# The last chunk of both output projections as a plain product by token blocks, in a diffusion block kernel

## The chip, the core and the metric

One core of a Trainium2 chip runs the whole program. The metric is the device time in microseconds of one execution; lower is better. TensorE (PE) multiplies, VectorE (DVE) and ScalarE (ACT) work on elements and on the accumulators in PSUM, GpSimd (POOL) works on elements in SBUF, and SyncE (SP) issues all transfers.

## What is computed

A block with 1024 latent tokens and 256 context tokens of width 1024, weights shared, modulation per token kind:

```
x = x + 0.5 * gate1 * swiglu(modulate(rmsnorm(x)), ff1_in, ff1_out)     # latent and context
mixer: one input projection, gated linear attention and gated MLP, one output projection
x = x + gate * mixer(modulate(rmsnorm(x)))                              # context only feeds states
x = x + 0.5 * gate2 * swiglu(modulate(rmsnorm(x)), ff2_in, ff2_out)     # latent only
out = rmsnorm(x) * final_g

def swiglu(y, w_in, w_out):
    gate, up = split(y @ w_in)
    return (silu(gate) * up) @ w_out                                    # 1024 -> 2 x 2816 -> 1024
```

## The kernel before

All values lie with features on the 128 partitions and tokens along the free axis: x[dt][tb] is feature tile dt (of 8) and token block tb (blocks 0 and 1 of 512 latent tokens, block 2 of 256 context tokens). Each operand of a product is split into a high and a low part in fp32r (an ACT copy and a subtraction, `split`, `hl`, `unit`), and each product is three matmuls: high by high, high by low, low by high.

Both products of an FFN are done by Winograd's variant of Strassen's scheme in 2 x 2 blocks: seven products instead of eight (`winograd`, products numbered 1, 2, 5, 7, 6, 3, 4). The rows of the left side are two halves of the weight (in the output projection feature tiles m and m + 4), the columns of the right side are token blocks 0 and 1, and the inner index is cut in two. `unit` (line 372) loads two weight tiles and makes the seven left operands with additions and subtractions on DVE (hidden part) or POOL (output projection). `combos` (L408 to L421) makes the combined right operands with four subtractions; `hl` (L429, L430) splits each.

`ffn` runs 22 hidden jobs first. `Hidden.end` finishes a pair of hidden tiles, and each pair's seven right operands are stored to DRAM (`hd`, L581). The output projection then reads them back (`hc`, L702) in CHUNKS of 1, 2, 2, 2, 2 and 2 pairs; each chunk has four jobs, one for each m. `Out.p1`, `p2`, `mid` and `end` add the products into sums in SBUF: `acc` for each feature tile and token block (L512), `us[m]` for the product that three of the four sums share. Up to the chunk before the last, product 6 goes to `us`, which `end` adds to the three sums there; in the last chunk it is added to each of the three directly. In the last chunk `finish` (L625) multiplies a sum by the gate and adds x, which it loads, and `tail` (`squares`, L461 and L463) squares the result on ACT and adds the square on DVE. So x of any token block is complete only when the last job has ended. In the first FFN the context's 256 tokens are a plain product in each job (`ctx`, L524 to L526), for two of the four jobs of the last chunk after all else.

After the first FFN `run` sums the squares over partitions for both blocks at once (`rstd_cols`: matmuls with ones, L265; a reciprocal square root in twelve small DVE steps, L279 and L247 to L255), spreads the result over the partitions (`spread`, L288) and norms block 0, block 1 and the context (`norm`: L327 on DVE, L329 and L331 on ACT, L334 on DVE or L332 on POOL). The mixer's products (L356 to L359) read the results. After the second FFN the same sums lead to sixteen outputs (L1399 and L1400 on ACT and POOL, or L1402 on DVE), which go to the result by L1404.

The order of instructions on each engine is worked out when the program is built: a planner takes instructions by priority (mostly the order of the code, `high_priority` earlier) as its own model of durations says that they are ready. At run time each engine works its list in order, and each waits for its operands. Buffers come from small pools: 32 of 1024 columns (`d`), 8 (`m`), 6 (`w`), 7 of 512 columns (`h`), and eight PSUM banks (`pg` 3, `po` 3, `pn` 2).

## Time and profile before

| what | value |
|---|---|
| time, median of 3 runs | 2215.16 us (2211.38 to 2219.64) |
| profiled execution, its own time | 2211.94 us |
| its span, first to last instruction | 2210.2 us |
| mean granted clock of PE | 0.951 of full speed |
| PE, DVE, ACT, POOL busy | 94%, 71%, 37%, 19% of the span |

The span is what the trace shows; 1.7 us of the execution's time lie around it. Times in the trace are counted from the start of the span. The first FFN's output projection ends at some 921 us, the mixer begins there, the second FFN's hidden part ends at some 1957 and its projection at 2180.

### The profile page before, as it was taken

How to read it: one execution, taken by the hardware profiler on the slowest of the kernel's cores; microseconds unless marked ns; L12 is line 12 of the kernel's file. 1: busy time of each engine (PE TensorE's matmuls, PEld its weight loads, DVE VectorE, ACT ScalarE, POOL GpSimd, SP SyncE). 2: the span in 40 equal slices, each digit the busy share in tenths (PEclk: the TensorE clock that was granted, in tenths of full speed). 3: DMA queues.
4: the chain of work that ended last, by engine and by line, in shares of the span. 5: the costliest groups of instructions: out<-in, count | busy, mean ns of one | idle time of the engine just before them, and what ended most of it. 6: DMA issues, size and time to landing. Idle time of an engine off the chain costs nothing.

```text
span 2210.2 us, 27546 instructions
## 1 busy us (share of the span) xinstructions
PE 2074.9 (94%) x10308; PEld 1722.6 (78%) x10308; DVE 1560.1 (71%) x2575; ACT 828.6 (37%) x1311; POOL 420.8 (19%) x245
## 2 busy tenths in 40 slices
PE   6799999999999999698999999996999999989995
PEld 2688888888878888577898787775788888867874
DVE  3976566666565689879877267779777776855587
ACT  3633333334351111275444234326344343441222
POOL 0000000000046565232111100110000000065772
PEclk9799999999999999899999986898999999999997
DMA  7033333233469776401111133541334343468851
GB/s 279 34 115 137 121 119 115 115 136 151 153 249 369 272 293 234 156 11 67 39 58 53 68 128 120 181 156 63 144 136 179 123 181 133 179 259 342 304 196 76
DMA packets 115878, 345.05 MB, mean 156 GB/s; under 512 B 12961, under 2 KB 15777, under 8 KB 115745
## 3 DMA queue, kind: packets, MB, share of 16 engines
q1 hardware_dynamic: 115744, 343.30, 42.2%
q8 instruction: 81, 1.33, 0.2%
q14 instruction: 53, 0.43, 0.1%
HBM read 237.87 MB, written 105.38 MB: 155 GB/s over the span
## 4 chain that ended last, share of the span: by engine, by line
PE 72%; DVE 15%; DMA 5%; POOL 3%; issue 3%; ACT 2%; SPq 0%; POOLq 0%; DVEq 0%; ACTq 0%
PE c L479 14%; PE a L479 13%; PE f L479 13%; PE b L479 7%; DVE acc L741 3%; PE sc L1056 2%; PE gc L526 2%; PE gc L525 2%; PE gc L524 2%; DVE acc L512 2%; DMA ar<-in_wb 1%; PE row L205 1%; PE st L265 1%; PE ogu L358 1%; PE ogu L356 1%
## 5 line engine op out<-in xcount | busy, mean ns | idle before, releaser
L384 POOL TENSOR_TENSOR gl<-raw,gh 128x1024 fp32r<-128x1024 f32 x22 | 54.1, 2461 | 1143.9 <-ACT gh L389 1129.6
L389 ACT ACTIVATE gh<-raw 128x1024 fp32r<-128x1024 f32 x66 | 70.0, 1060 | 198.6 <-PE c L479 83.7
L168 DVE SCALAR_TENSOR_TENSOR junk<-ar,cr 128x512 bf16<-128x512 f32 x160 | 111.9, 700 | 35.4 <-DMA ar<-in_wb 26.3
L393 ACT ACTIVATE sh<-s 128x1024 fp32r<-128x1024 f32 x66 | 69.7, 1057 | 170.8 <-PE a L479 93.2
L429 ACT ACTIVATE hl<-g 128x512 fp32r<-128x512 f32 x110 | 67.5, 626 | 158.8 <-DVE g L512 152.2
L479 PE MATMUL f<-hl,uh 128*128 128x512 f32 x528 | 126.8, 389 | 0.0
L479 PE MATMUL c<-hl,sh 128*128 128x512 f32 x352 | 110.9, 392 | 11.4 <-ACT hl L429 9.2
L479 PE MATMUL a<-hl,gh 128*128 128x512 f32 x352 | 113.6, 400 | 8.1 <-ACT hl L429 5.6
L479 PEld LDWEIGHTS f<-hl,uh 128*128 128x128 f32 x528 | 99.1, 188 | 20.6
L479 PE MATMUL b<-hl,gh 128*128 128x512 f32 x352 | 111.5, 393 | 1.0 <-ACT hl L429 1.0
L479 PE MATMUL f<-hl,th 128*128 128x512 f32 x352 | 110.1, 390 | 1.3 <-ACT hl L429 1.3
L479 PE MATMUL a<-hl,sh 128*128 128x512 f32 x352 | 110.2, 393 | 1.0 <-ACT g L552 1.0
L479 PE MATMUL c<-hl,th 128*128 128x512 f32 x352 | 109.0, 391 | 0.1
L741 DVE SCALAR_TENSOR_TENSOR acc<-z,par,acc 128x945 f32<-128x945 f32 (+2 forms) x64 | 95.5, 1511 | 12.0 <-ACT acc L763 10.9
L512 DVE TENSOR_TENSOR u<-c,u 128x512 f32<-128x512 f32 x44 | 30.3, 689 | 98.4 <-ACT u L562 98.4
L430 DVE TENSOR_TENSOR hl<-g,hl 128x512 fp32r<-128x512 f32 x110 | 76.9, 715 | 32.3 <-ACT hl L429 32.2
L142 POOL TENSOR_TENSOR wl<-raw,wh 128x1024 fp32r<-128x1024 f32 x20 | 52.3, 2614 | 222.5 <-ACT wh L141 213.7
L479 PEld LDWEIGHTS c<-hl,sh 128*128 128x128 f32 x352 | 66.2, 189 | 26.7 <-ACT hl L429 9.8
L384 DVE TENSOR_TENSOR sl<-s,sh 128x1024 fp32r<-128x1024 f32 x44 | 53.9, 1224 | 45.7 <-PE gc L525 21.9
L479 PEld LDWEIGHTS a<-hl,gh 128*128 128x128 f32 x352 | 66.6, 193 | 22.1 <-ACT hl L429 6.1
L512 DVE TENSOR_TENSOR acc<-f,acc 128x512 f32<-128x512 f32 x88 | 60.3, 688 | 28.3 <-PE f L479 23.0
L479 PEld LDWEIGHTS b<-hl,gh 128*128 128x128 f32 x352 | 67.0, 190 | 15.7 <-ACT hl L429 1.8
(330 smaller groups left out, 6211.6 us busy)
## 6 DMA issues: line engine op xcount, KB each, us to landing
hd<-hl SPq DMA_DIRECT2D x154, 512.0 KB, 3.7
hc<-hd SPq DMA_DIRECT2D x154, 512.0 KB, 7.7
ar<-in_wb SPq DMA_DIRECT2D x112, 256.0 KB, 3.1
raw<-in_ff1i SPq DMA_DIRECT2D x44, 512.0 KB, 3.8
raw<-in_ff2i SPq DMA_DIRECT2D x44, 512.0 KB, 4.7
raw<-in_ff1o SPq DMA_DIRECT2D x22, 512.0 KB, 6.2
raw<-in_ff2o SPq DMA_DIRECT2D x22, 512.0 KB, 5.4
raw<-in_wa SPq DMA_DIRECT2D x16, 512.0 KB, 10.0
```

The lines of the kernel that those rows point to most:

```text
L142: eng.tensor_tensor(out=lo[:, :n], in0=src[:, :n], in1=hi[:, :n].bitcast(F32), op=ALU.subtract)
L168: i = nc.vector.scalar_tensor_tensor(out=self.junk, in0=w, scalar=1.0, in1=cbc[j], op0=ALU.mult, op1=ALU.mult, accum_out=acc[:, h, dt, j:j ...
L384: sub = lambda o, x, y: eng.tensor_tensor(out=o, in0=x, in1=y, op=ALU.subtract)
L389: nc.scalar.activation(gh, g, AF.Copy)
L393: nc.scalar.activation(sh, s, AF.Copy)
L429: nc.scalar.activation(t[:, :512], src, AF.Copy)
L430: nc.vector.tensor_tensor(out=t[:, 512:], in0=src, in1=t[:, :512].bitcast(F32), op=ALU.subtract)
L479: mm = lambda x, y, start, stop: nc.tensor.matmul(ps, x, y, start=start, stop=stop, skip_group_check=more)
L512: tt = lambda eng, o, x, y, op: eng.tensor_tensor(out=o, in0=x, in1=y, op=op)
L524: nc.tensor.matmul(ps, hi[:, c], mh, start=i == 0, stop=False)
L525: nc.tensor.matmul(ps, hi[:, c], ml, start=False, stop=False)
L741: self.nc.vector.scalar_tensor_tensor(out=o, in0=zv[:, r0 + dr:r1 + dr, c0 + dc:c1 + dc], scalar=self.par[:, tap:tap + 1], in1=o, op0=ALU. ...
```

## The change

Three things are changed in both FFNs. The last chunk (hidden pairs 9 and 10) leaves the Winograd scheme: `last` multiplies it plainly, all eight feature tiles for token block 0, then all eight for block 1, then, in the first FFN, the context. Its weights are only split into high and low parts (`halves`), its right operands are the four blocks themselves, so that pairs 9 and 10 store four operands instead of seven and make no combinations. The sums of the other chunks are multiplied by the gate and added to x before the last chunk or in its first half (`finish` and `fold_u` for block 0 in the chunk before the last, for block 1 among block 0's tiles), and each tile of the last chunk is multiplied by the gate and added to x from PSUM (`more`). After each token block its own norm follows (`done`): in the first FFN the mixer's norm of that block, in the second the final norm and the outputs. x is loaded and its copy stored by pairs of feature tiles for each block. The sums' tiles hold two feature tiles of one block instead of one feature tile of both.

```diff
+    def halves(self, src, eng, new):
+
+        nc = self.nc
+        r = {}
+        for x, (i, j) in zip(src, ((1, 2), (0, 4))):
+            x = self.load(x)
+            hi, lo = new("vh", F32R), new("vl", F32R)
+            with self.tc.high_priority():
+                nc.scalar.activation(hi, x, AF.Copy)
+                eng.tensor_tensor(out=lo, in0=x, in1=hi.bitcast(F32), op=ALU.subtract)
+            r[i], r[j] = (hi[:, :512], lo[:, :512]), (hi[:, 512:], lo[:, 512:])
...
+        def tail(dt, tb):
+            sq = self.sv("sq") if tb in accs else self.tile(self.sb, 512, "ar", "acc")
+            nc.scalar.activation(sq, self.x[dt][tb], AF.Square)
+            if tb in accs:
+                nc.vector.tensor_tensor(out=accs[tb], in0=accs[tb], in1=sq, op=ALU.add)
+            else:
+                accs[tb] = sq
...
+        pairs0 = NF // 2 - CHUNKS[-1]
...
+                    if pair >= pairs0:
+                        out(5, b12)
+                        out(7, b22)
+                        return
                     layer.combos(b11, b12, b21, b22, out)
...
             def p2(s, b):
-                i = add(s.acc(s.m, 0), b, False)
+                i = add(xsum(s.m, 0), b, False)
                 if after_out:
                     after_out(s.j, i)
-                if s.last:
-                    s.finish(s.m, 0)
+                if s.fold:
+                    finish(s.m, 0)
                 if yc:
-                    if s.put_off:
-                        later.append(s.ctx)
-                    else:
-                        s.ctx()
+                    s.ctx()
 
             def mid(s, a, c, f):
                 m = s.m
                 if s.one:
                     us[m] = layer.h("u")
-                if s.last:
-                    for dt, tb in ((m + 4, 1), (m, 1), (m + 4, 0)):
-                        add(s.acc(dt, tb), a, False)
-                else:
-                    add(us[m], a, s.one)
-                add(s.acc(m + 4, 1), c, s.one)
-                add(s.acc(m + 4, 1), f, False)
-                if s.last:
-                    s.finish(m + 4, 1)
+                add(us[m], a, s.one)
+                add(xsum(m + 4, 1), c, s.one)
+                add(xsum(m + 4, 1), f, False)
 
             def end(s, c, f):
                 m = s.m
-                add(s.acc(m, 1), c, s.one)
-                add(s.acc(m + 4, 0), f, s.one)
-                if s.chunk == len(CHUNKS) - 2:
-                    for dt, tb in ((m, 1), (m + 4, 0), (m + 4, 1)):
-                        o = s.acc(dt, tb)
-                        tt(nc.vector, o, o, us[m], ALU.add)
-                if s.last:
-                    s.finish(m, 1)
-                    s.finish(m + 4, 0)
-                    tail(m)
-                    tail(m + 4)
+                add(xsum(m, 1), c, s.one)
+                add(xsum(m + 4, 0), f, s.one)
+                if s.fold:
+                    fold_u(m + 4, 0)
+                    finish(m + 4, 0)
+
...
+        def fold_u(dt, tb):
+            o = xsum(dt, tb)
+            tt(nc.vector, o, o, us[dt % 4], ALU.add)
...
+        def more(x, ps, dt, j):
+            nc.vector.scalar_tensor_tensor(out=x, in0=ps, scalar=gates()[:, dt, j:j + 1], in1=x,
+                                           op0=ALU.mult, op1=ALU.add)
...
+        def finish(dt, tb):
+
+            if (dt // 2, tb) not in xt:
+                xt[dt // 2, tb] = load_x(dt // 2, tb)
+            self.x[dt][tb] = xt[dt // 2, tb][:, dt % 2 * 512:dt % 2 * 512 + 512]
+            more(self.x[dt][tb], xsum(dt, tb), dt, 0)
...
+        def last():
+            kd = CHUNKS[-1]
+            ws = [self.halves(w2[NFO - kd + q], nc.gpsimd, (self.w, self.m)[q % 2 == 0]) for q in range(kd)]
+            tiles = [(q * (4 // kd) + m, i, ws[q], m * kd * P) for q in range(kd) for m in range(4 // kd)
+                     for i in range(2)]
+            rows = lambda w, i, col: [(*w[r], slice(col + k * P, col + k * P + P)) for r in ((1, 2), (0, 4))[i]
+                                      for k in range(kd)]
+            for tb in range(2):
+                right = []
+                for i in ((1, 2), (5, 7))[tb]:
+                    for pair in range(pairs0, NF // 2):
+                        t = self.d("hc", F32R)
+                        nc.sync.dma_start(t.bitcast(F32), hd[pair, names.index(i)])
+                        right.append((t[:, :512], t[:, 512:]))
+                for m, i, w, col in tiles:
+                    dt = m + 4 * i
+                    ps = self.po("o") if i else self.pg("o")
+                    plain(ps, rows(w, i, col), right)
+                    more(self.x[dt][tb], ps, dt, 0)
+                    tail(dt, tb)
+                    if tb == 0:
+                        fold_u(dt, 1)
+                        finish(dt, 1)
+                    elif yc:
+                        finish_c(dt)
+                done(tb)
+            if yc:
+                cs = []
+                for pair in range(pairs0, NF // 2):
+                    t = self.m("cc", F32R)
+                    nc.sync.dma_start(t.bitcast(F32), hc[pair])
+                    cs.append(t)
+                right = [(t[:, h:h + 256], t[:, h + 256:h + 512]) for h in (0, 512) for t in cs]
+                for m, i, w, col in tiles:
+                    dt = m + 4 * i
+                    if i == 0:
+                        pc = self.po("oc")
+                    ps = pc[:, i * 256:i * 256 + 256]
+                    plain(ps, rows(w, i, col), right)
+                    more(self.x[dt][2], ps, dt, 1)
+                done(2)
...
-        for ci, kd in enumerate(CHUNKS):
+        for ci, kd in enumerate(CHUNKS[:-1]):
...
         self.winograd(jobs)
-        for ctx in later:
-            ctx()
+        last()
...
+        def done1(tb):
+            if "c2" not in late:
+                late["c2"] = self.norm_coef(3, C_N2, 2, "2")
+            self.alloc_y(y2, tb)
+            r = self.rstd(part(2)) if tb == 2 else self.rstd_cols([accs[tb]], 512, 1.0 / 1024.0)
+            self.norm(part(tb), late["c2"], y2, r, pool=True)
...
-        r = self.rstd_cols([accs[0], accs[1]], 512, 1.0 / 1024.0)
-        for tb in range(2):
-            self.alloc_y(y2, tb)
-            self.norm(part(tb), c2, y2, r[:, 4 * tb:4 * tb + 4], pool=True)
-        self.alloc_y(y2, 2)
-        self.norm(part(2), c2, y2, self.rstd(part(2)), pool=True)
...
+        def done2b(tb):
+            bc = self.spread(self.rstd_cols([accs[tb]], 512, 1.0 / 1024.0), 4)
+            b0 = self.h("bc")
+            nc.scalar.activation(b0, bc, AF.Copy)
+            for k in range(NK):
+                g = self.par[:, C_FG + k:C_FG + k + 1]
+                o = self.h("out")
+                if tb and k % 3 == 2:
+                    nc.scalar.activation(o, self.x[k][tb], AF.Identity, scale=g)
+                    nc.gpsimd.tensor_tensor(out=o, in0=o, in1=b0, op=ALU.mult)
+                else:
+                    nc.vector.scalar_tensor_tensor(out=o, in0=self.x[k][tb], scalar=g, in1=bc,
+                                                   op0=ALU.mult, op1=ALU.mult)
+                nc.sync.dma_start(a["out"][k, :, tb * 512:tb * 512 + 512], o)
+
         accs = {}
         self.ffn(mov, None, a["ff2i"], a["ff2o"], gates2, load_x2, None, self.squares(accs),
-                 self.ada_todo((8,), 1, 1, 16))
...
+                 done2b, self.ada_todo((8,), 1, 1, 16))
```

## Rows read from the trace of the kernel before

**Rows 1.** The page's busy time of each engine over the whole span.

```profile
PE 2074.9 (94%) x10308; PEld 1722.6 (78%) x10308; DVE 1560.1 (71%) x2575; ACT 828.6 (37%) x1311; POOL 420.8 (19%) x245
```

**Rows 2.** Busy time by stretches: from:to and length, engines with instructions, clock, DMA.

```profile
core 0: us, PE busy (x) PEld busy (x) DVE busy (x) ACT busy (x) POOL busy (x), PEclk, DMA share, GB/s
...
888.00:921.00 33.00, 27.40 (x132) 23.07 (x132) 30.87 (x44) 9.05 (x12) 10.06 (x5) 0.90 0.43 149
921.00:947.00 26.00, 9.71 (x38) 8.75 (x39) 20.33 (x42) 11.64 (x19) 4.39 (x3) 0.65 0.36 122
947.00:985.00 38.00, 38.00 (x167) 30.88 (x167) 27.09 (x51) 28.26 (x55) 12.31 (x9) 0.97 0.02 7
...
1010.00:1060.00 50.00, 41.01 (x196) 33.28 (x195) 38.52 (x51) 30.09 (x60) 8.38 (x4) 0.97 0.17 57
...
1954.00:1965.00 11.00, 6.00 (x16) 4.41 (x16) 9.74 (x16) 7.16 (x13) 3.65 (x4) 0.75 0.55 218
...
2180.00:2210.00 30.00, 7.30 (x32) 6.98 (x32) 16.46 (x34) 8.13 (x13) 7.52 (x6) 0.58 0.36 140
```

**Rows 3.** Busy time by stretches, PE first: matmuls reading hc, then those writing oc.

```profile
864.77:921.00 56.23, 41.96 (x168) 32.40 (x168) 0.94 0.52 178
2134.96:2180.00 45.04, 41.68 (x169) 32.01 (x167) 0.96 0.16 64
...
862.60:864.77 2.17, 2.15 (x18) 2.10 (x17) 0.00 (x0) 0.00 (x0) 1.00 0.87 282
862.60:921.00 58.40, 12.76 (x96) 12.38 (x95) 2.23 (x6) 0.00 (x0) 0.94 0.54 182
```

**Rows 4.** Timeline of PE: start, length, instruction, count; six products back to back.

```profile
2178.45 1.52 PE L479 MATMUL f<-hc,uh 128*128 128x512 f32 x6
```

**Rows 5.** Timeline of PE: gaps in both FFNs, in brackets idle time and what ended it.

```profile
638.66 0.58 PE L524 MATMUL oc<-cc,gh 128*128 128x256 f32 x1 [2.16 <-DVE u L512]
...
893.42 1.22 PE L479 MATMUL f<-hc,th 128*128 128x512 f32 x2 [5.75 <-ACT th L396]
...
932.16 3.57 PE L265 MATMUL st<-ones,acc 128*128 128x1 f32 x16 [11.34 <-DVE acc L463]
...
1960.30 1.22 PE L479 MATMUL c<-hc,th 128*128 128x512 f32 x2 [3.88 <-ACT acc L607]
```

**Rows 6.** Timeline of the end: the final norm's steps and the last outputs.

```profile
2186.86 3.55 PE L265 MATMUL st<-ones,acc 128*128 128x1 f32 x16 [6.88 <-DVE acc L463]
2190.44 0.17 DVE L279 TENSOR_SCALAR r<-st 128x8 f32<-128x8 f32 x1 [3.13 <-PE st L265]
...
2192.97 3.75 PE L288 MATMUL bc<-ident,r 128*128 128x128 f32 x16 [2.56 <-DVE r L255]
...
2196.76 2.06 DVE L1402 SCALAR_TENSOR_TENSOR out<-x,par,bc 128x512 f32<-128x512 f32 x3 [3.94 <-PE bc L288]
...
2204.15 2.21 DVE L1402 SCALAR_TENSOR_TENSOR out<-x,par,bc 128x512 f32<-128x512 f32 x3 [0.55 <-DMA out_x<-out]
```

**Rows 7.** Groups of instructions, 2135 to 2190: count, busy us, mean ns, idle before.

```profile
L625 DVE SCALAR_TENSOR_TENSOR x<-acc,hg,x 128x512 f32<-128x512 f32 x16 | 12.7, 803 | 0.0
...
L512 DVE TENSOR_TENSOR acc<-a,acc 128x512 f32<-128x512 f32 x16 | 10.3, 680 | 0.0
L461 ACT ACTIVATE sq<-x 128x512 f32<-128x512 f32 x14 | 8.3, 625 | 24.1 <-DVE x L625 22.7 <-DVE acc L463 1.4
```

**Rows 8.** A DVE addition beside POOL (timeline), and the page's group of POOL subtractions.

```profile
2140.18 2.84 POOL L384 TENSOR_TENSOR tl<-s,th 128x1024 fp32r<-128x1024 f32 x1
2140.69 2.88 DVE L512 TENSOR_TENSOR acc<-acc,u 128x512 f32<-128x512 f32 x1
...
L384 POOL TENSOR_TENSOR gl<-raw,gh 128x1024 fp32r<-128x1024 f32 x22 | 54.1, 2461 | 1143.9 <-ACT gh L389 1129.6
```

**Rows 9.** Groups of the mixer's norm on DVE, 864 to 960.

```profile
L327 DVE SCALAR_TENSOR_TENSOR t<-x,A,bc 128x512 f32<-128x512 f32 x16 | 10.9, 738 | 2.2 <-PE bc L288 2.2
L334 DVE SCALAR_TENSOR_TENSOR y<-t,mods,y 128x512 fp32r<-128x512 f32 x8 | 7.4, 959 | 0.0
```

95 lines of the change are left out of this document (30 added, 65 removed).

## The prediction, made before the result was known

> **What bounds the kernel now.** I read the busy shares first. TensorE (PE) is busy 94% of the span [rows 1], so what it does not do is confined to a few places, and added products cost their full pitch wherever it is saturated. The busy times by stretch show where it is not saturated: [rows 2] has six stretches around the two feed-forward networks (FFN). In 888 to 921 us, the last chunk of the first output projection, PE works 27.40 of 33 us at a granted clock of 0.90 while VectorE (DVE) is full, 30.87 of 33. In 921 to 947, the norm between that projection and the mixer, PE works 9.71 of 26 at 0.65. In 1954 to 1965, between the hidden part and the projection of the second FFN, it works 6.00 of 11. In 2180 to 2210, the norm at the end, 7.30 of 30. From 947 on it is full again (38.00 of 38). Then I read what ended PE's gaps [rows 5]: 5.75 us for the split of the last weight (th, ScalarE, ACT), 11.34 us for the last sum of squares on DVE, 3.88 us for an ACT copy queued behind the pair splits, and 2.16 us for a DVE addition at the same place of the first FFN. So the places which the change touches are bounded by DVE, ACT and the chain of the norm, not by products.
>
> **Products.** Before, the last chunk has 4 jobs of 7 products, 2 rows and 3 matmuls: 168. A plain product has 8 tiles, 2 token blocks, 4 rows and 3 matmuls: 192, so 24 more per FFN. Six back-to-back matmuls take 1.52 us and one lasts 0.39 [rows 4], so the pitch is (1.52 - 0.39) / 5 = 0.226 us: 24 of them cost 5.4 us per FFN, 10.9 in all, on PE. The context products are the same 96, at 2.17 / 18 = 0.12 us [rows 3].
>
> **Second FFN, last chunk and end.** The last 168 matmuls start at 2134.96 and end at 2179.98 [rows 3]: 45.0 us for 168 x 0.226 = 38.0 us of work; 7.0 us are waits and half clock. From there to the end of the span are 30.2 us, together 75.2. After:
> - 192 x 0.226 = 43.4 us of products.
> - The norm of block 0 now lies among the products of block 1. Its column sums and its broadcast are half of those for both blocks, (3.55 + 3.75) / 2 = 3.65 us of PE [rows 6]. They now count, where they lay in a gap before.
> - Waits: 2 us, my choice between 0 and the 7.0 of before. DVE's load per tile is a gated addition 0.75 and a square sum 0.68 [rows 7], in block 0 also the fold of u (0.68) and the first gated addition of block 1 (0.75): 22.9 us against 21.7 of PE in block 0; in block 1 11.4 plus the chain of the norm 2.5 and eight outputs of some 0.75, 19.9 us against 25.3. Before, it was 36 additions, 16 gated additions and 14 square sums, some 46 us in a stretch of 45, which is why PE waited. PE can run ahead by six PSUM banks, so block 0's 1.2 us of excess disappears in block 1.
> - The end for block 1 alone: gated addition, square, sum 0.75 + 0.63 + 0.68 and some 0.3 between engines, 2.4; column sums 1.8; from their end to the broadcast 2192.97 - 2190.44 = 2.5; broadcast 1.9; six DVE outputs at 2.06 / 3 = 0.69, 4.1 (the other two go over ACT and GpSimd (POOL) beside them); from the last DVE output, 2204.15 + 2.21, to the end of the span, 3.8 [rows 6]. Sum 16.5. Before, sixteen outputs through seven buffers had to wait for each other's stores; block 0's eight stores now leave on SP's queue during block 1, where nothing else is queued but loads issued earlier.
>
> Sum 43.4 + 3.65 + 2 + 16.5 = 65.6, gain 9.6 us (4.6 if all 7.0 us of waits stay, 11.6 with none).
>
> **First FFN and the way into the mixer.** After 862.60 before has 168 products and 96 of the context [rows 3], 38.0 + 11.5 = 49.5 us, and needs until 932.16 - 11.34 = 920.8: 8.7 us of waits, 5.75 of them for the last weight's split [rows 5]. That split is replaced: two copies and two subtractions of 128x1024 per weight (some 2 x 2.46 us of POOL [rows 8]) instead of eight or nine. After: 43.4 + 11.5 + 2 x 3.65 for the norms of blocks 0 and 1 + 4 us of waits (between 0 and 8.7; the nearest row is again the second FFN's last chunk, but three norms share DVE here) = 66.2, so the mixer's products start at 862.6 + 66.2 = 928.8. Before they ran steadily from 947, less some five matmuls that lay before it (38 matmuls in that stretch less 32 of sums and broadcast [rows 2, 6]), so 945.9. Gain 17.1 us. The cover for the norm of block 1 is the 11.5 us of context products and block 0's own mixer products. Block 1 needs 2.4 + 1.8 + 2.5 + 1.9 and on DVE eight steps of 0.74 and four low halves of some 0.7 [rows 9] (the other four go to POOL), about 17 us, against 11.5 + the first 10.9 us of mixer products that read block 0 only. Without this cover some 5 us would come back.
>
> **Mixer.** Its front is shared by PE and DVE: in 1010 to 1060 PE works 41.01 of 50 us [rows 2], behind the convolutions on DVE. These need both blocks; both are ready earlier relative to the first product than before. Between 0 and those 9 us can be gained: I take 3, as PE also waits there for gate chains on ACT.
>
> **Hidden part.** For the last two pairs of each FFN 8 subtractions, 6 copies, 6 low parts and 6 stores of 512 KB fall away. In the steady part PE hides all of them: nothing. At the turn into the projection they stand before what PE waits for: 16 matmuls (3.6 us) took 11 us in 1954 to 1965 [rows 2], so 7.4 us are lost, and the first FFN has 2.16 [rows 5]. I take 4.4 and 1.6, 6 in all (0 to 9.6).
>
> **Moved at no cost.** x of block 0 is now loaded (four DMAs) and gated in the chunk before the last, eight DVE additions of 0.75; in exchange eight folds of u of 0.68 leave that chunk. There the products cover DVE. If x lands late, DVE waits at the head of its queue with the PSUM evacuations behind it, and PE after six banks; that is in the waits above.
>
> **Sum.** 9.6 + 17.1 + 3 + 6 = 35.7 us off the profiled execution's 2211.94 gives 2176.2. The median of the three runs is 3.2 us above that execution, so I predict 2178.
>
> **Rivals.**
> - *More than that (chance 0.16).* No waits, all of the mixer's 9 and of the turns' 9.6 us: 2211.9 - (11.6 + 21.1 + 9 + 9.6) = 2160.6. For it: all that it asks is that DVE keeps up, and its work in a last chunk falls from some 46 us to 34. Against: every stage before has some waits.
> - *DVE takes PE's place in the first FFN (0.21).* Block 1's stretch now has the sums of squares, the folds, and the norm with its POOL operations at once. A DVE addition that lay beside POOL subtractions of 2.84 us took 2.88 us instead of 0.68 [rows 8]. With eight such hits, 8 x 2.2 = 17.6 us, the 17.1 are gone: 2211.9 - 15.6 - 3 = 2193 at best and 2196 without the mixer's. Against: a norm has four POOL steps per block, and block 0's stand beside gated additions that read PSUM.
> - *A convoy in the queues, the slower case (0.10).* The planner writes each engine's order ahead. If DVE's queue has the norm's first step (it waits for the column sums) ahead of the evacuations of block 1, while PE's queue has those sums behind more than six tiles of block 1, PE fills its banks and all wait. Each of the three norms (two here, one in the second FFN) would cost up to six tiles, 6 x 2.7 = 16 us: 2176 + 48 = 2224. It decides once the sums stand more than a few tiles late; at half of it the result is 2200. For it: the gaps of 11.34 and 6.88 us before the sums are of this kind of place [rows 5, 6]. Against: their cause before was only that nothing else was left to do.
> - *PE's occupancy alone counts (0.03).* The added products show in full and the gaps move elsewhere: 2211.9 + 10.9 = 2222.8. Against it stand the gaps of [rows 2], where PE is no bound.
>
> On the second rival: the Trainium skill, "SBUF — State Buffer", section "SBUF: two separate sides", says that DVE operations with two SBUF inputs and GpSimd operations take one port pair by turns, and that the loser is blocked for the other's whole instruction. The row of 2.88 us agrees with it; by that rule the second rival holds wherever a norm's POOL steps meet the sums of squares.
>
> On the last rival: the Trainium skill, "Perfetto Trace Analysis", section "Identifying the Most-Contended Engine", says to optimize first the engine with the highest occupancy, which here is PE, and the change does the reverse. The stretches above do not bear it out for these places.
>
> **How the numbers follow.** The forecast (2166 to 2192) has 0.50. Something over 0.5% of 2215, 11 us, is what a measurement of this kernel can tell from no change. Faster by more than that: the forecast, the first two rivals, and no part of the others: 0.87. Of the convoy's 0.10 and the last rival's 0.03 I put 0.07 within 0.5% (a convoy at one or two norms) and 0.06 beyond it. The range of 8 in 10 takes the forecast, the better case down to 2160, and DVE's case up to 2202.
>
> **What would show it.** Right: 924 + 24 matmuls per projection; PE busy at clock 1.0 through the stretch between projection and mixer, with the column sums of block 0 in the middle of block 1's products; from the last product to the end some 17 us; no wait of PE for a weight's split. Wrong: PE idle in front of the sums with banks full; DVE additions of over 2 us in the first FFN's block 1; PE gaps in the mixer's front that take back what the norm gave; the turn at 1954 unchanged.

## The result, and the profile after

The changed kernel takes 2186.7 us (median of 4 runs, 2186.1 to 2193.1) against 2214.7 before: a ratio of 0.9876 with a 95% interval of 0.986 to 0.9892, some 28 us. The forecast was 2178 with 2160 to 2202. The sign, the range and the size hold, but the gain is a quarter smaller than forecast, and the stages show that a third of it does not come from where I put it.

The page of the changed kernel begins with the busy times, the answer to [rows 1]. There are the 48 matmuls more, at a share of 95%:

```profile
span 2184.2 us, 27435 instructions
PE 2068.8 (95%) x10356; PEld 1717.9 (79%) x10356; DVE 1528.0 (70%) x2535; ACT 812.2 (37%) x1286; POOL 380.6 (17%) x215
```

Totals hide the stages, so I cut both traces (one profiled execution of each kernel) at products that both kernels have: the last context product of the first hidden part, the first product of `vs` behind the mixer's front, the last of the states (`ds`), the first of the mixer's output projection (`wo`), the first of the second hidden part, the last in it that reads a gate weight's low part (`a<-hl,gl`), and the last product of all. The last cut but one lies 23 and 26 us ahead of the hidden part's own last product (which ends at 1950.9 us before, not at some 1957, and at 1937.1 after), because the projection's first products stand among the hidden part's last ones. The row behind it therefore holds the whole turn from hidden part to projection. In us:

| stage | before | after | difference | forecast |
|---|---|---|---|---|
| start and first hidden part | 624.8 | 625.9 | +1.1 | 0 |
| first projection, norm, mixer's front | 479.1 | 469.3 | -9.8 | -21.7 (17.1 + 3 + 1.6) |
| mixer up to the states | 130.7 | 130.7 | 0 | 0 |
| mixer's tail | 162.2 | 152.8 | -9.4 | 0 |
| mixer's output projection | 107.2 | 108.4 | +1.2 | 0 |
| second hidden part, to that cut | 423.5 | 424.1 | +0.6 | 0 |
| its rest, turn and second projection | 252.5 | 254.3 | +1.8 | -0.3 |
| end | 30.2 | 18.9 | -11.3 | -13.7 |

(The forecast's second FFN is its 9.6 and 4.4, divided here: 16.5 us of end instead of 30.2, and the rest ahead of it.) The first row is chance: over all kernels traced, which are all but alike up to there, it lies between 624.8 and 631.7. So below I compare stages and not instants.

Two rows do not fit the forecast: the norm behind the first projection gave less than half, and the mixer's tail, which the change does not touch, gave 9.4 us.

The busy times by stretch of the changed kernel, the answer to [rows 2], show the first:

```profile
core 0: us, PE busy (x) PEld busy (x) DVE busy (x) ACT busy (x) POOL busy (x), PEclk, DMA share, GB/s
888.00:921.00 33.00, 26.33 (x112) 21.92 (x111) 24.80 (x47) 12.43 (x20) 6.31 (x4) 0.84 0.41 148
...
894.50:900.50 6.00, 3.52 (x15) 3.43 (x16) 1.97 (x12) 0.00 (x0) 0.00 (x0) 0.50 0.96 299
...
921.00:947.00 26.00, 26.00 (x168) 23.52 (x167) 18.76 (x38) 11.85 (x19) 7.86 (x4) 1.00 0.19 71
...
2165.00:2185.00 20.00, 4.07 (x18) 3.42 (x16) 9.79 (x24) 3.54 (x6) 2.50 (x2) 0.61 0.35 134
```

The stretch from 921 to 947, where PE was busy 9.71 us, is full now. But 888 to 921 is no better than it was: 26.33 of 33 us, at a lower clock, 0.84. The timeline of PE says why (start, length, instruction, count, idle time before it and what ended it); its last two rows are the same steps in the second FFN:

```profile
889.93 0.39 PE L541 MATMUL o<-hc,vl 128*128 128x512 f32 x1
894.55 1.86 PE L266 MATMUL st<-ones,acc 128*128 128x1 f32 x8 [4.24 <-DVE acc L476]
898.85 2.07 PE L289 MATMUL bc<-ident,r 128*128 128x128 f32 x8 [2.44 <-DVE r L256]
900.58 0.77 PE L539 MATMUL o<-hc,vh 128*128 128x512 f32 x1
...
2148.33 0.95 PE L266 MATMUL st<-ones,acc 128*128 128x1 f32 x8
2157.66 1.05 PE L289 MATMUL bc<-ident,r 128*128 128x128 f32 x8
```

In the second FFN the column sums and the broadcast of block 0 stand among block 1's products, 30 and 67 of them in, and PE waits for neither. In the first FFN the planner has written them directly behind block 0's 96 products and ahead of block 1's 96. PE, which works its list in order, stands in front of them for 4.24 and 2.44 us and does them at the lower of its two clock levels, 1.2 GHz: 0.50 in the row from 894.5 to 900.5, where it has sums and broadcast. Block 1's operands are late there too. The SyncE queue:

```profile
886.75 2.42 SPq L1300 DMA_DIRECT2D xd<-x  x2
890.97 2.43 SPq L1301 DMA_DIRECT2D xd<-x  x2
893.51 2.05 SPq L714 DMA_DIRECT2D hc<-hd  x4
```

The four loads of block 1 (`hc`) stand behind the eight stores of block 0's x (`x_spill`), each of which waits for its gated addition. They landed between 898.8 and 902.9 us, and PE goes on with block 1 at 900.6, so another order on PE alone would not have helped much.

### The profile page after: what moved, and what is told of

The parts are those of the page before. It is cut to its first block, busy times and chain, and to the rows that moved or that the text cites. A ratio compares the mean times of both kernels' runs of the same rounds, so it can differ in the third digit from the quotient of the medians.

```text
span 2184.2 us, 27435 instructions
## 1 busy us (share of the span) xinstructions
PE 2068.8 (95%) x10356; PEld 1717.9 (79%) x10356; DVE 1528.0 (70%) x2535; ACT 812.2 (37%) x1286; POOL 380.6 (17%) x215
## 4 chain that ended last, share of the span: by engine, by line
PE 76%; DVE 16%; DMA 3%; issue 2%; ACT 2%; POOL 0%; SPq 0%; DVEq 0%; ACTq 0%
PE a L492 14%; PE c L492 14%; PE f L492 14%; PE b L492 7%; DVE acc L791 3%; PE sc L1106 3%; PE gc L541 2%; PE gc L540 2%; PE gc L539 2%; DVE acc L526 2%; PE row L206 1%; DVE hl L444 1%; PE ogu L357 1%; PE ogu L359 1%; PE ogu L360 1%
## 5 line engine op out<-in xcount | busy, mean ns | idle before, releaser
L384 POOL TENSOR_TENSOR s<-raw 128x512 f32<-128x512 f32 x18 | 24.2, 1346 | 1132.1 <-DMA cc<-hc 602.2
L443 ACT ACTIVATE hl<-g 128x512 fp32r<-128x512 f32 x106 | 64.3, 626 | 157.2 <-DVE g L526 152.8
L492 PE MATMUL c<-hl,sh 128*128 128x512 f32 x352 | 111.0, 393 | 11.6 <-ACT hl L443 9.5
L791 DVE SCALAR_TENSOR_TENSOR acc<-z,par,acc 128x945 f32<-128x945 f32 (+2 forms) x64 | 93.2, 1478 | 11.6 <-ACT acc L813 10.5
L492 PEld LDWEIGHTS a<-hl,sh 128*128 128x128 f32 x352 | 66.7, 190 | 15.8 <-ACT g L567 1.3
```

What stands on the lines that cost most here:

```text
L443: nc.scalar.activation(t[:, :512], src, AF.Copy)
L492: mm = lambda x, y, start, stop: nc.tensor.matmul(ps, x, y, start=start, stop=stop, skip_group_check=more)
L791: self.nc.vector.scalar_tensor_tensor(out=o, in0=zv[:, r0 + dr:r1 + dr, c0 + dc:c1 + dc], scalar=self.par[:, tap:tap + 1], in1=o, op0=ALU. ...
```

## The experiments

In front of the runs stands what each theory expected. The stages below are measured as in the table above, on one profiled execution of each kernel. "Loss" is the time that passed less the matmuls started, at 0.2266 us for 512 columns and 0.1206 for 256; "the turn" is the stretch of a projection's first two chunks, in which the hidden part's last products also lie. A table of all runs closes the section.

**One FFN at a time.** The former projection and norm stand beside the new ones under another name, and one FFN calls them:

```diff
-        self.ffn(mov, yc, a["ff1i"], a["ff1o"], ..., self.squares(accs),
-                 done1, self.ada_todo((2, 3, 4), 2, 3, 16))
+        self.ffn_old(mov, yc, a["ff1i"], a["ff1o"], ..., self.squares_old(accs),
+                 self.ada_todo((2, 3, 4), 2, 3, 16))
```

> The change in the second FFN alone; the first FFN and its norm stand as before. Theory (from the two traces: of the 26 us between the spans, 9 lie behind the first product of the second FFN): 2214.7 - 9 = 2206, between 2203 and 2208; the hidden part's turn at about 1954 gives 4, the last chunk and the end together 4 to 5. Rival (the forecast's own terms 9.6 + 4.4): 2201 or less. Second rival (part of the 9 us is only another order of the planner's): above 2210.

Measured 2203.7 us, ratio 0.9948 (0.9931 to 0.9964), 11.6 us less, in the theory's range, near its lower end. Its second projection and end take 254.6 and 19.1 us, as in the changed kernel; its mixer's tail takes 162.2, as before.

> The change in the first FFN alone; the second FFN and the end stand as before. Theory A (what the mixer's tail gained between 1286 and 1400 us, 8.5 us at another clock, belongs to the order that the planner writes for this kernel, and comes again): 2214.7 - 17 = 2198, between 2195 and 2201. Theory B (those 8.5 us are chance of that execution): 2206, between 2204 and 2209. The forecast's terms (17.1 + 3 + 1.6): 2193.

Measured 2198.8 us, ratio 0.9926 (0.9907 to 0.9945), 16.5 us less: theory A. The tail takes 152.8 us again. The two parts add up to the whole, 11.6 + 16.5 = 28.1, and the tail's 9.4 us belong to the first FFN's half; they are no chance of one execution.

**The cover that was missing.** The norm of block 0 is issued inside block 1's tiles, so that block 1's operands are allotted and loaded before it:

```diff
-                for m, i, w, col in tiles:
+                for t, (m, i, w, col) in enumerate(tiles):
+                    if tb and t == 3:
+                        done(0)
...
-                done(tb)
+                if tb:
+                    done(1)
```

> The changed kernel, with the norm of block 0 issued behind the third tile of block 1, in both FFNs, so that its column sums stand among block 1's products on TensorE's queue and block 1's operands are allotted before the normalized x. Theory (the step of the forecast that failed in the first FFN is the cover of that norm: TensorE stood 4.2 and 2.4 us and then ran at half clock): about 9 us less than the changed kernel, 2178, and TensorE without a gap between block 0 and the mixer. Rival (the front of the mixer, whose convolutions fill VectorE, takes back what arrives earlier): 2184 to 2187, with a gap of the same 9 us between 1000 and 1060. Second rival (the norm's steps on VectorE and GpSimd now hold up block 1's additions): 2187 to 2192.

Measured 2185.3 us, ratio 0.9861 (0.9845 to 0.9878): by its total the rival. By its stages it is not. The busy times show PE without a break where it stood before:

```profile
888.00:921.00 33.00, 33.00 (x166) 28.03 (x165) 26.00 (x47) 13.92 (x23) 4.30 (x3) 1.00 0.36 127
921.00:947.00 26.00, 26.00 (x158) 23.14 (x157) 19.97 (x39) 15.62 (x27) 11.22 (x6) 1.00 0.25 77
```

First projection, norm and front take 456.9 us, 12.4 less than in the changed kernel and 22.2 less than before, where the forecast had 21.7. The mixer's tail takes 163.3 us instead of 152.8 and eats 10.5 of the 12.4. So the forecast of this place was right for a kernel in which the cover exists, and an untouched stage decides the total.

**Without a norm of its own for each block.**

```diff
-                done(tb)
+            for tb in range(2):
+                done(tb)
```

> The changed kernel, but with both blocks' norms behind both blocks' products (in the first FFN ahead of the context's products, in the second at the end): the plain product without its own norm for each block. Theory: the second FFN loses what the norm of block 0 among block 1's products gave, 30.2 - 18.9 us of the end less the 3.65 us of sums and broadcast that then need no place among the products, 7 to 8 us; the first FFN neither gains nor loses much, as its norm of block 0 was not covered: 2194, between 2191 and 2198. Rival (the own norm is what all of the gain rests on): 2207 or more.

Measured 2187.7 us, ratio 0.9875 (0.986 to 0.989), better than either theory. The second FFN loses 4.8 us (253.5 + 24.5 against 254.3 + 18.9), less than I had put. The first gains 7.1 (462.2 against 469.3), which I had put at nothing: a norm that PE waits for in the middle of the projection is worse than one behind it that the context's products cover. (Of the 7.1, 1.6 lie in the chunk before the last, whose loss is 2.7 us here and 4.3 in the changed kernel.) So in the form in which the change was made, its own norm for each block gives next to nothing over both FFNs.

**What the chunk before the last pays.** In the changed kernel PE loses 7.2 us in that chunk of the second FFN and 4.3 in that of the first, where it lost 0.7 and 0.1 before and I had put nothing. The other kernels that leave this chunk as the change has it lose 6.7 to 7.6 and 2.4 to 4.5. The stretch of the kernel before first, then busy times by stretch, and the timelines of VectorE and GpSimd, of the changed kernel:

```profile
2096.00:2135.00 39.00, 38.76 (x171) 31.52 (x170) 26.91 (x37) 7.53 (x8) 28.57 (x17) 1.00 0.65 243
```

```profile
2080.00:2090.00 10.00, 10.00 (x46) 8.29 (x45) 8.05 (x12) 1.06 (x1) 6.39 (x5) 1.00 0.79 261
2090.00:2100.00 10.00, 8.01 (x35) 5.98 (x33) 10.00 (x9) 2.96 (x3) 9.41 (x4) 1.00 0.55 198
2100.00:2110.00 10.00, 8.02 (x23) 6.38 (x24) 8.37 (x13) 1.06 (x1) 2.51 (x2) 0.66 0.49 160
```

```profile
2092.88 0.68 DVE L526 TENSOR_TENSOR acc<-f,acc 128x512 f32<-128x512 f32 x1
2093.48 2.29 DVE L686 SCALAR_TENSOR_TENSOR x<-acc,hg,x 128x512 f32<-128x512 f32 x1
2095.69 2.87 DVE L526 TENSOR_TENSOR acc<-acc,u 128x512 f32<-128x512 f32 x1
2098.48 0.68 DVE L526 TENSOR_TENSOR acc<-a,acc 128x512 f32<-128x512 f32 x1
2099.08 2.24 DVE L686 SCALAR_TENSOR_TENSOR x<-acc,hg,x 128x512 f32<-128x512 f32 x1
...
2092.40 2.82 POOL L420 TENSOR_TENSOR vl<-raw,vh 128x1024 fp32r<-128x1024 f32 x1 [0.59 <-ACT vh L419]
2095.18 2.82 POOL L385 TENSOR_TENSOR sl<-s,sh 128x1024 fp32r<-128x1024 f32 x1
2097.97 2.81 POOL L385 TENSOR_TENSOR tl<-s,th 128x1024 fp32r<-128x1024 f32 x1
```

From 2092.4 to 2100.8 us GpSimd subtracts without a pause, a fourth subtraction ends 0.6 us ahead of that, and each fold (`acc<-acc,u`) and gated addition (`x<-acc,hg,x`), whose operands all lie in SBUF, that meets one ends only half a microsecond behind the subtraction's end, as the pair of [rows 8] showed: 2.24 to 2.87 us instead of 0.68 and 0.75. The additions between them, which take one operand from PSUM (`f`, `a`), keep their 0.68. The Trainium skill, "SBUF — State Buffer", section "SBUF: two separate sides", says that of a VectorE operation with two SBUF inputs and a GpSimd operation the one that starts first has their shared port pair for its whole instruction while the other is fully blocked; the trace agrees with it. VectorE is full for 10 us with 9 operations, and PE waits 1.9 and 2.0 us for an `acc` and falls to a clock of 0.66: 3.9 us of waits and 0.34 x 10 us of clock make up the loss. Beyond that, the planner has drawn most of the work here: 14 of the 16 gated additions and 11 of the 12 folds of the second FFN start before this chunk's last product ends, though the source has eight of either in the last chunk.

*Moving the work in the source.*

```diff
-                if s.fold:
-                    fold_u(m + 4, 0)
-                    finish(m + 4, 0)
...
+                    if tb == 0:
+                        if i:
+                            fold_u(dt, 0)
+                        finish(dt, 0)
                     plain(ps, rows(w, i, col), right)
```

> The changed kernel, with the loading of x, the gated addition and the fold of u for block 0 issued in the last chunk's block 0 and no longer in the chunk before it (8 gated additions and 4 folds per FFN). In the trace of the changed kernel these operations of two SBUF operands lie beside back-to-back GpSimd subtractions and last up to 2.9 us, and TensorE loses 7.2 us there in the second FFN and 4.3 in the first. Theory (that pile-up is the price that the forecast put at nothing): TensorE loses under 1 us in the chunk before the last of each FFN, and block 0 becomes VectorE's: 31.6 us of VectorE work against 21.7 of products, of which block 1 takes back some 5; so about 11.5 - 2 x 4.5 = 2 us less in all, 2184 (2180 to 2189). Rival (the loss of the chunk before the last does not come from these operations): it stays, and block 0's surplus comes on top, 2195 or more.

Measured 2189.9 us, ratio 0.9886 (0.9872 to 0.9901), but it tells nothing of the theories: 14 gated additions and 11 folds stand in front of the chunk's end as before. The planner undid the edit; the loss is 7.5 and 4.5 us. A place in the source is no place on the engine.

*Taking GpSimd's part away.*

```diff
-                eng.tensor_tensor(out=lo, in0=x, in1=hi.bitcast(F32), op=ALU.subtract)
+                nc.scalar.activation(lo, x, AF.Copy)
```

> The changed kernel without the GpSimd subtraction of the last two weights: their low parts are plain copies of the weight by ScalarE (this leaves out part of the computation), four of 128x1024 per FFN. GpSimd's other subtractions (two per unit of the chunk before) stay. Theory (GpSimd's subtractions stretch VectorE's operations of two SBUF operands): of the 7.2 and 4.3 us that TensorE loses in the chunk before the last about half goes, 2181 (2179 to 2184), and VectorE's operations over 1.5 us become fewer there. Rival (VectorE's operations are long for a reason of their own): 2186 to 2188, durations as before.

Measured 2176.6 us, ratio 0.9827 (0.9808 to 0.9847), more than the theory: the losses are not halved but gone, 0.01 and 0.06 us. Stretches and groups of this kernel in the same chunk (the groups from 2088 to 2102: count, busy us, mean ns):

```profile
2090.00:2100.00 10.00, 10.00 (x46) 8.29 (x45) 10.00 (x14) 3.91 (x4) 4.83 (x2) 1.00 0.60 202
2100.00:2110.00 10.00, 10.00 (x45) 8.27 (x45) 9.86 (x16) 2.88 (x3) 0.39 (x1) 1.00 0.57 203
```

```profile
L526 DVE TENSOR_TENSOR acc<-acc,u 128x512 f32<-128x512 f32 x5 | 4.9, 1003 | 0.0
L686 DVE SCALAR_TENSOR_TENSOR x<-acc,hg,x 128x512 f32<-128x512 f32 x5 | 4.7, 933 | 0.0
```

VectorE is just as full, but with 14 and 16 operations per 10 us instead of 9 and 13. Two subtractions beside the drawn work cost PE nothing; four almost in a row cost it 7.2 us.

*GpSimd's subtraction on VectorE instead.*

```diff
-            ws = [self.halves(w2[NFO - kd + q], nc.gpsimd, (self.w, self.m)[q % 2 == 0]) for q in range(kd)]
+            ws = [self.halves(w2[NFO - kd + q], nc.vector, (self.w, self.m)[q % 2 == 0]) for q in range(kd)]
```

> The changed kernel, with the last two weights' low parts (four subtractions of 128x1024 per FFN) on VectorE in place of GpSimd: some 4 x 1.22 = 4.9 us of VectorE more per FFN, and none of GpSimd's last subtractions beside its folds and gated additions. Theory (what costs is GpSimd's subtraction beside VectorE's operations of two SBUF operands, and not VectorE's load): 2180 (2177 to 2183), TensorE's loss in the chunk before the last falls from 7.2 and 4.3 us to 2 to 4 and 1 to 2, since VectorE there has some 10 us free. Rival (VectorE's load alone decides): 2186 to 2190.

Measured 2180.5 us, ratio 0.9838 (0.9821 to 0.9854), as the theory has it. The losses are 1.1 and 0.7 us although VectorE has four subtractions more. VectorE's load alone is not what costs; GpSimd's subtractions beside it are needed too.

*Holding the work where the source has it*, by an order that the planner must keep:

```diff
-                    more(self.x[dt][tb], ps, dt, 0)
+                    here = more(self.x[dt][tb], ps, dt, 0)
                     tail(dt, tb)
                     if tb == 0:
-                        fold_u(dt, 1)
-                        finish(dt, 1)
+                        layer.after(here, fold_u(dt, 1), finish(dt, 1))
```

> The changed kernel, with an order that keeps each fold of u and gated addition of block 1 behind the addition of block 0's product of the same tile, where the source has them; the planner of the changed kernel had drawn most of them (6 of 8 gated additions, 7 of 8 folds) into the chunk before the last, onto the back-to-back GpSimd subtractions. Theory (what the forecast put at nothing was costly because all of it was drawn together in front of GpSimd's subtractions): TensorE's 7.2 and 4.3 us there fall to 1 to 3 us each, block 0 stays covered by its products (22.9 us of VectorE against 21.7): 2181 (2178 to 2184). Rival (the subtractions alone are enough to hold up VectorE): 2185 to 2188. Second rival (VectorE then is late in block 0 and the norm waits): above 2188.

Measured 2181.3 us, ratio 0.9853 (0.9828 to 0.9877): the theory. Now 9 gated additions and 5 folds of the second FFN start before the chunk ends, and the loss is 0.01 us there and 1.7 in the first; the last chunk that follows in the second FFN loses nothing. The chunk's stretches, and PE's wait in the first FFN:

```profile
2080.00:2090.00 10.00, 10.00 (x46) 8.29 (x45) 6.44 (x9) 1.26 (x2) 7.67 (x6) 1.00 0.80 302
2090.00:2100.00 10.00, 10.00 (x46) 8.28 (x45) 9.83 (x10) 2.87 (x3) 8.29 (x4) 1.00 0.38 124
...
892.75 1.87 PE L266 MATMUL st<-ones,acc 128*128 128x1 f32 x8 [5.47 <-DVE acc L476]
```

GpSimd's four subtractions are still there, with a pause of 1.7 us in their middle, and VectorE still finishes only 10 operations in the second stretch, but PE does not wait: there is less for VectorE to do. So the loss needs both, the work drawn together and the subtractions beside it; either one taken away brings it to 1.1 us or less in that FFN. The forecast's reckoning of VectorE (22.9 us against 21.7 in block 0) then holds for the order that it assumed. In the first FFN the 2.5 us saved are lost again: the uncovered norm waits 5.47 us for its last sum instead of 4.24.

**The turn from the hidden part to the projection.**

```diff
-                    if pair >= pairs0:
-                        out(5, b12)
-                        out(7, b22)
-                        return
```

> The changed kernel, with the four subtractions, six operands' splits and stores of the last two pairs computed as before the change, though nobody reads three of the seven. Theory (the turn from the hidden part to the projection gains 3.7 us in the second FFN because these stand ahead of what TensorE waits for, and nothing in the first): 3.7 us more, 2190 (2188 to 2192), with TensorE's loss between the hidden part and chunk 1 back at 11 us in the second FFN. Rival (the turn is bound by the loads of the operands): 2186 to 2188.

(Block 1 of its last chunk then reads combinations where the product needs the plain halves; sizes and counts are those of the changed kernel.) Measured 2194.9 us, ratio 0.9911 (0.9895 to 0.9928), 8.1 us more than the changed kernel and more than expected. At the second turn PE loses 10.9 us instead of 7.0, as the theory says (before: 11.2). A further 4.8 us, where the changed kernel loses 1.5, go in the chunk behind the turn, where PE waits up to 2.8 us for a weight's split (`sh`). At the first turn it is 11.4 instead of 9.3. Those extra losses have no match in the kernel before (8.5 at the first turn, 2.3 behind the second), so I do not count them as the change's gain.

**The mixer's tail.** One more place for the norm, behind the fifth tile instead of the third (`t == 5`), for which the planner writes a different order of products in the tail (in the second FFN, too, the norm stands there):

> As the kernel with the norm of block 0 inside block 1, but behind the fifth tile of block 1; the planner then writes another order of the scan's and the projection's products in the mixer's tail (from the end of the states to the first product of the output projection). Theory (that tail takes 152.8 or some 163 us by the order of its products alone, at another granted clock, whatever the norm does): the front gains 10 to 13 us as before, and the whole is 2174 to 2178 where the tail comes out at about 153 us and 2184 to 2188 where it comes out at 163. Rival (the tail takes back whatever arrives earlier, because it waits for something that does not move): 2185 to 2188, with the sum of front and tail unchanged against the changed kernel.

Measured 2177.2 us, ratio 0.9825 (0.981 to 0.9839). The total and the tail, 151.3 us, are the theory's. The front takes 461.0, a gain of 8.3 us and not the 10 to 13 expected; `wo` is 2.8 us shorter than in the changed kernel, for which I have no cause. The tail does not take back what comes early.

Then the kernel before, with one edit outside the change with which the planner writes the first 623 of the tail's 764 to 780 traced products in that same order (by tile names and shapes):

```diff
-        self.norm(part(2), c2, y2, self.rstd(part(2)), pool=True)
+        self.norm(part(2), c2, y2, self.rstd(part(2)))
```

> The kernel before, unchanged but for one thing: the low parts of the context's norm (four of 128x256) are taken on VectorE and not on GpSimd. Nothing of the change is in it; but the planner then writes the order of the mixer's tail as it stands in the kernel with the norm behind the fifth tile. Theory (the tail takes 151 to 153 us or 162 to 163 by the order of its products and by the clock granted to it, and 9.4 of the changed kernel's 28 us are this by-product): 2214.7 - 10.5 = 2204 (2201 to 2207), the tail at 151 to 153 us with the half clock after its middle some 10 us shorter, and everything ahead of and behind it as before. Rival (the tail was shorter because its inputs were ready earlier, by the earlier norm): 2212 to 2217, tail at 162.

Measured 2201.1 us, ratio 0.9936 (0.9921 to 0.9951), 14 us less than the kernel before, without any of the change. The first projection, norm and front take 479.9 us (479.1), the tail 150.6 instead of 162.2. Busy times of the five stretches from 110 us behind the last product of the states on, of the kernel before, of this one and of the changed one:

```profile
1344.50:1354.50 10.00, 8.70 (x53) 7.05 (x52) 8.30 (x18) 10.00 (x22) 0.00 (x0) 0.88 0.62 196
1354.50:1364.50 10.00, 10.00 (x34) 7.55 (x33) 7.19 (x22) 3.75 (x9) 2.79 (x2) 0.50 0.57 170
1364.50:1374.50 10.00, 10.00 (x35) 7.94 (x34) 6.57 (x13) 1.18 (x2) 0.00 (x0) 0.50 0.32 107
1374.50:1384.50 10.00, 10.00 (x36) 7.98 (x36) 0.00 (x0) 1.28 (x2) 0.00 (x0) 0.50 0.06 22
1384.50:1394.50 10.00, 10.00 (x68) 8.64 (x69) 2.33 (x6) 1.81 (x3) 0.00 (x0) 0.58 0.07 22
```

```profile
1346.50:1356.50 10.00, 10.00 (x71) 8.26 (x69) 7.03 (x17) 9.95 (x24) 1.45 (x1) 1.00 0.69 211
1356.50:1366.50 10.00, 10.00 (x55) 8.19 (x55) 9.60 (x26) 1.86 (x3) 2.09 (x2) 0.85 0.55 184
1366.50:1376.50 10.00, 10.00 (x33) 7.42 (x34) 2.01 (x6) 1.94 (x4) 0.00 (x0) 0.50 0.17 53
1376.50:1386.50 10.00, 10.00 (x74) 9.64 (x76) 5.04 (x12) 1.15 (x2) 0.00 (x0) 0.50 0.17 54
1386.50:1396.50 10.00, 9.48 (x89) 6.84 (x86) 10.00 (x23) 2.90 (x5) 0.00 (x0) 0.95 0.26 79
```

```profile
1335.80:1345.80 10.00, 10.00 (x69) 8.11 (x68) 7.60 (x17) 10.00 (x22) 0.00 (x0) 1.00 0.67 197
1345.80:1355.80 10.00, 10.00 (x55) 7.74 (x54) 7.48 (x22) 3.94 (x9) 2.87 (x2) 0.88 0.54 183
1355.80:1365.80 10.00, 10.00 (x36) 7.98 (x35) 7.00 (x15) 1.28 (x2) 0.00 (x0) 0.50 0.31 94
1365.80:1375.80 10.00, 10.00 (x68) 9.41 (x70) 6.10 (x17) 1.80 (x3) 0.00 (x0) 0.50 0.41 131
1375.80:1385.80 10.00, 8.74 (x95) 6.86 (x91) 10.00 (x29) 2.52 (x4) 0.00 (x0) 0.92 0.40 138
```

The column after POOL is the clock. Before, it is at the lower level (0.50) from the second row to the middle of the fifth; in the other two it falls a row later and is back in the fifth. One less the clock, times 10 us and summed over the five rows, is 20.4 us before against 12.0 in both others, 8.4 of the 9.4 us. In the kernel before PE stood 1.30 us at 1350.3, waiting for a state of the scan, just before the clock fell; the other two have no such gap there. The same gap, 117 us behind the states, stands in all three kernels whose tail takes over 162 us, that is before, second FFN only and norm behind tile 3, and in none of the eleven others:

```profile
1351.61 1.74 PE L1056 MATMUL sc<-x 64*128 64x128 f32 x8 [1.30 <-DVE S L1075]
1357.34 2.06 PE L1342 MATMUL sc<-x 64*128 64x128 f32 x8 [1.49 <-DVE S L1361]
1334.95 1.90 PE L1109 MATMUL sc<-x 64*128 64x128 f32 x8 [1.44 <-DVE S L1128]
```

In these three the clock falls at 117.1 to 117.5 us behind the states, in the others at 125.3 to 130.5. That the gap brings the fall forward is argued from these rows, not tried by itself. What the runs show is that the tail goes by its order: the two kernels with the order of before take 162.2 us each, the six with the very order of the changed kernel 152.7 to 152.9, and the six with other orders 149.7 to 152.6, but for one of 163.3. The order does not settle it to the last microsecond: the kernel with the norm behind tile 5 and the one with both mended have the same order and take 151.3 and 149.7.

**Both mended.** The norm of block 0 behind the fifth tile in the first FFN, and the folds and gated additions held in place in both:

> The changed kernel with the two things that the runs so far gave: in the first FFN the norm of block 0 behind the fifth tile of block 1 (in the second as the change has it), and in both the folds of u and gated additions of block 1 behind the addition of block 0 of the same tile. Theory (the forecast's two wrong steps were these places, and they are independent): against the kernel with the norm behind the fifth tile (2177.2), 6.7 us less in the chunk before the last of the second FFN, 1 to 2.5 in the first, 1 at the end: 2168 (2165 to 2171), with the mixer's tail at 151 to 153 us as its order of products is that kernel's. Rival (VectorE's work kept back in block 0 makes the norm of block 0 late, as it did in the first FFN when its gap before the sums grew from 4.2 to 5.5 us): 2172 to 2178.

Measured 2168.2 us (5 runs), ratio 0.9778 (0.9758 to 0.9797): the theory's number, and 18.5 us below the changed kernel. The loss in the chunk before the last is 1.8 and 0.01 us, and the front takes 458.6 us, 2.4 less than with the norm behind tile 5, all as expected. The tail, 149.7 us, lies below the theory's 151 to 153.

All runs, stages in us (`wo` from its first to its last product; it varies by 5 us, and I did not look for the cause; "second projection" is the row "its rest, turn and second projection" of the table above):

| kernel | median us | first projection to front | tail | wo | second projection | end |
|---|---|---|---|---|---|---|
| before | 2214.7 | 479.1 | 162.2 | 103.5 | 252.5 | 30.2 |
| changed | 2186.7 | 469.3 | 152.8 | 104.6 | 254.3 | 18.9 |
| second FFN only | 2203.7 | 478.1 | 162.2 | 103.7 | 254.6 | 19.1 |
| first FFN only | 2198.8 | 467.7 | 152.8 | 107.1 | 251.3 | 30.2 |
| norm behind tile 3 | 2185.3 | 456.9 | 163.3 | 102.8 | 255.5 | 19.4 |
| norms late | 2187.7 | 462.2 | 152.9 | 107.0 | 253.5 | 24.5 |
| finish moved in the source | 2189.9 | 469.8 | 152.8 | 106.9 | 255.1 | 19.1 |
| low parts by ScalarE | 2176.6 | 460.9 | 152.9 | 106.6 | 247.1 | 18.3 |
| combinations kept | 2194.9 | 472.5 | 152.0 | 104.9 | 261.7 | 19.1 |
| norm behind tile 5 | 2177.2 | 461.0 | 151.3 | 101.8 | 253.6 | 20.7 |
| before, other order | 2201.1 | 479.9 | 150.6 | 103.5 | 252.3 | 29.8 |
| held in place | 2181.3 | 469.9 | 152.6 | 104.1 | 247.6 | 19.4 |
| low parts by VectorE | 2180.5 | 466.1 | 152.7 | 106.8 | 248.9 | 19.1 |
| both mended | 2168.2 | 458.6 | 149.7 | 101.7 | 248.0 | 19.7 |

## Why the prediction was right, and where it was not

The time lay in the range, and the forecast of a gain was right. Of its steps:

- *Products, +10.9 us.* Right: 948 matmuls per projection, and behind the chunk before the last, the 171 products left of the last chunk's 192, from 2124.53 to 2165.33, need 38.7 us at their pitch and the norm's 2.0 us, 40.8 in all. PE does not wait in them at all, where I had put 2 us and the kernel before had 7.0; the norm takes 0.95 + 1.05 us among the products, where I had put 3.65, since its rows in [rows 6] stood at half clock (0.50 in both). VectorE's share was reckoned with 0.75 us for a gated addition, where [rows 7] shows a mean of 803 ns; that is under 1 us for a block and decides nothing.
- *The second FFN's end, 16.5 us.* Too low by 2.4. The sums come 3.7 us behind the last product and not 2.4, as VectorE writes block 0's last outputs ahead of block 1's last three additions, and from the broadcast's end it takes 8.9 us and not 7.9, of which VectorE waits 0.7 for ScalarE's copy of the broadcast:

```profile
2169.06 1.69 PE L266 MATMUL st<-ones,acc 128*128 128x1 f32 x8 [3.73 <-DVE acc L476]
2173.27 2.05 PE L289 MATMUL bc<-ident,r 128*128 128x128 f32 x8 [2.52 <-DVE r L256]
...
2175.99 4.25 DVE L1447 SCALAR_TENSOR_TENSOR out<-x,par,bc 128x512 f32<-128x512 f32 x6 [2.86 <-ACT bc L1439]
```

- *The second turn, 4.4 us.* Right: the loss falls from 11.2 to 7.0. The first turn, 1.6 us, gave nothing: 8.5 before, 9.3 after, and 7.3 to 9.4 in the other kernels with the new hidden part of the first FFN (without the one that keeps the combinations).
- *"Moved at no cost."* This is the step that failed: it cost 7.2 and 4.3 us. I weighed the number of operations and not their neighbours, and I took the source's place for the place on VectorE. With the work held in place the second FFN's loss is 0.01 us and the first's 1.7; with the last weights' subtractions taken from GpSimd and the work left where it was, they are 0.01 and 0.06.
- *The first FFN's norm, 17.1 us, and the mixer's 3.* The gain that came is 9.8. For a kernel with the cover the mechanism and the sum were right (22.2 us against 21.7 with the turn's 1.6; when the mixer's 200th `z` product starts, 18.0 of it are there against 18.7 forecast, and 4.2 come behind that against 3). But the changed kernel doesn't have the cover, and it gains 9.9 us up to that product and nothing behind it: the sums of block 0 stand ahead of block 1's products. I listed an order of the planner as a rival (the convoy), but with the sums too late; here they are too early, and PE stands for them. Why the planner writes it so I did not settle: it goes away when block 1's operands are allotted ahead of the normalized x.
- *The mixer's tail.* Not in the forecast at all, 9.4 us of gain. The other stages together fell 19.3 us short of the forecast (11.9 at the first projection and front, 5.1 from the second hidden part on, 2.3 elsewhere); the tail hides half of that. That the total lies so near the forecast is luck, and it looks better than the reasoning was.
- *The last step of the sum.* 2176.2 plus the 3.2 us between the median and the profiled execution are 2179.4, not 2178. Nothing hangs on it.

Of the rivals, VectorE blocked by GpSimd was the right mechanism at the wrong place: not in the first FFN's norm but in the chunk before the last of both, and at 11.5 us instead of 17.6. That PE's occupancy alone counts was refuted: its share rose to 95% and the time fell.

Against a kernel before with the better order in its tail (2201.1) the change is worth 14 us and not 28.

## What to carry to other kernels

Where a planner writes the queues, a cover or a place in the source counts only once the order on the engine shows it; hold it with an explicit order if it matters. Before work of two SBUF operands is called free on VectorE, look at what GpSimd does in that stretch, not at VectorE's share alone. And compare kernels stage by stage, with a control whose only edit is outside the change: here one such edit moved the time by 14 us.

## What I had not expected of the hardware

The granted clock in the mixer's tail repeats with the order of the products from kernel to kernel: two with the order of before have 162.2 us each, six with the changed order 152.7 to 152.9. A short gap on PE can come with a far larger loss: the 1.30 us in the tail of the kernel before go with 8.4 us more of clock lost. The gaps of 4.24 and 2.44 us at the first norm came with a clock of 0.84 over 33 us, where the kernel with the covered norm had 1.00; that is another 5 us (0.16 x 33), part of it in the gaps themselves. In no run was a gap the only thing changed, so that it causes the fall is not shown. And the port shared by VectorE and GpSimd did its harm only where much work met much work: in one stretch of 10 us VectorE finished 9 operations and PE lost time, in another (the work held in place) it finished 10 beside GpSimd's subtractions and PE lost none.
